# Input stage of a hybrid decoder layer: later scaling of constants, no GpSimd subtractions, casts on ScalarE, one product in fp32, a new order

## The chip, the cores and the metric

The kernel runs on one core of one Trainium2 chip. The metric is device time in microseconds; the time before is the median of three runs, 1275.76 us.

## The reference, cut to what matters

One layer of a decoder trunk with two token mixers side by side. The part that the change touches is the first: layer norm of the 16 meta tokens and 1024 tokens, and the first three of the products with `w_in`.

```python
D_MODEL, SEQ, N_META = 1024, 1024, 16                  # 1040 tokens in all
def reference(x, meta_tokens, in_ln_g, in_ln_b, ..., w_in, b_in, ...):
    h = jnp.concatenate([meta, x], axis=1)
    h = layer_norm(h, in_ln_g, in_ln_b)                # the input stage
    h = hybrid_layer(h, ...)
    return h[:, N_META:]

def hybrid_layer(h, ...):
    z = h @ w_in + b_in
    q, k, v, c_in, gates = jnp.split(z, ...)           # 512, 128, 128, 1024, 2048 columns
    a = swa_sink_attention(q, k, v, attn_sinks, rel_bias)
    y_attn = a @ w_attn_proj
    ...                                                # gated conv branch, merge, norm, conv FFN, norm
```

## The kernel before, in words

**Products in three parts.** Nearly every fp32 product is made of three TensorE products of rounded operands. An operand is split in a high part (a cast to the rounded type fp32r) and a low part (the operand minus the high part, again rounded); low x high, high x high and high x low are summed in PSUM. So each operand costs a cast and a subtraction before TensorE can use it. A product can also be made directly in fp32 from the raw operands, which takes no cast and no subtraction.

**The input stage.** Tokens come as nine tiles of up to 128 rows: the meta tokens (`xm`, tile -1) and eight tiles of x. `stat` takes the mean and variance of a tile on VectorE (L440, L441; `half_stat`, L452, does half a tile), `table` the reciprocal square root on ScalarE (L459), `newton` refines it in four small VectorE steps (L465 to L468), `norm` normalizes the tile on VectorE (L478) or ScalarE (L480). Statistics go in four sets: (-1), (0, 1), (2, 3, 4), (5, 6, 7). Three token groups of 272, 384 and 384 columns follow: (-1, 0, 1), (2, 3, 4), (5, 6, 7). For each group and each of eight channel chunks k, `turns` transposes on TensorE (L498, with the identity matrix, which comes in the tile `coll`), `scaled` applies gain and bias on ScalarE (L504, `FA` or `tm`, with columns of the tile `colr`), and `parts` makes the high part on VectorE (L514, into `RHO`) and the low part on VectorE (L519) or GpSimd (L517, into `RHC`).

**The first products.** `first` holds three weight tiles of 128 columns, in this order of indices: 0 the keys (column tile 4), 1 the values (column tile 5), 2 the first queries (column tile 0). `wsplit0(i)` splits one: a cast on ScalarE (L526), then a subtraction on GpSimd (L528; all three calls ask for it). `z_first(g, tiles, *ks)` makes the products of group g with the named tiles for chunks ks, three TensorE products for each k (L550), or one fp32 product where `raw` is set (L547: the keys of the first group). `evac` empties PSUM on ScalarE: keys (L379), values (L386), queries (L395 and L397, and a VectorE subtraction, L398); the stores of keys and of the queries' high part are issued from ScalarE's queue (L128).

**What sets the order.** Three lists, `dv`, `ac` and `pe`, pin the order of VectorE, ScalarE and TensorE in this stage to the order in which the program text issues the work; the sequence is written out by hand (L563 on). Evacuations are not pinned; they have a rank (`RK_EVAC`), and a scheduler places them. Loads are issued from SyncE (SP) in an order set by ranks; raw weights have two buffers (`wr`), and the fourth fill waits until one of the first is done with. The pools that matter: four PSUM buffers for transposes, four for normalized tiles, five for `tm`.

**Behind the stage.** The next weight tile (`wt_c1`, column tile 11) is split by ScalarE (L304) and VectorE (L307) into the buffer that the key weights leave, and the long run of products in `z_group` starts (L342, L345, L346). Beside it VectorE works off the residual rows (`residual`, L293 and L294), and later the convolution.

**The constants.** Three small VectorE steps scale constants in `colr` (L247, L249, L252). They are unpinned, and stand in the program text ahead of the stage.

Of the kernel before, what the change touches and what calls it, by code (L numbers as in the profile page):

```python
# [26 lines left out]
OP = mybir.AluOpType  # L27
# [10 lines left out]
HD = 64  # L38
# [74 lines left out]
def tile_hybrid_layer(  # L113
# [3 lines left out]
    nc = tc.nc  # L117
# [12 lines left out]
    def f32(ap):  # L130
        return ap.bitcast(F)
# [115 lines left out]
    nc.vector.tensor_scalar(qb, colA[:, 0:4], HD ** -0.5, None, OP.mult)  # L247

    nc.vector.tensor_scalar(colA[:, 10:30], colA[:, 10:30], 0.5, None, OP.mult)  # L249
    half_ = constr.tile([P, 1], F, name="half")  # L250
    nc.vector.memset(half_, 0.5)
    nc.vector.tensor_scalar(nsink, sink, -1.0, None, OP.mult)  # L252
# [28 lines left out]
    def h0(k, hl, a, b):  # L281
        return (RHO, RHC)[hl][:, k * T + a:k * T + b]
# [159 lines left out]

    half_st = {}
# [26 lines left out]
    def norm(t, j, on_dve):  # L470
        x_, n = src_of(j)
        i = tokens[t].index(j)
        mv, t_, r_, m_ = norms[t]
        xns[j] = sp.tile([P, D], F, name="xn", tag="xn", bufs=4) if j >= 0 else xm
        to = xns[j] if j >= 0 else xm[96:]
        for a in range(0, D, 512):
            if on_dve:
                dv(V.tensor_scalar(to[:, a:a + 512], x_[:, a:a + 512], r_[:n, i:i + 1], m_[:n, i:i + 1], OP.mult, OP.add))  # L478
            else:
                ac(nc.scalar.activation(to[:, a:a + 512], x_[:, a:a + 512], AF.Identity, bias=m_[:n, i:i + 1],  # L480
                                        scale=r_[:n, i:i + 1]))
        later.append((x_, mv[:n, i, 0:1], r_[:n, i:i + 1], n, j))
# [24 lines left out]
    def parts(g, *ks, hi_act=(), on_pool=()):  # L507
        a, b = HG[g]
        for k in ks:
            tm = tms[g, k]  # L510
            if k in hi_act:
                ac(nc.scalar.copy(h0(k, 0, a, b), tm))
            else:
                dv(V.tensor_copy(h0(k, 0, a, b), tm))  # L514
            x_ = (h0(k, 1, a, b), tm, f32(h0(k, 0, a, b)), OP.subtract)
            if k in on_pool:
                nc.gpsimd.tensor_tensor(*x_)  # L517
            else:
                dv(V.tensor_tensor(*x_))  # L519
# [4 lines left out]
    def wsplit0(i, on_pool=False):  # L524
        hi, lo, raw = first[i]
        ac(nc.scalar.copy(hi, raw))  # L526
        x_ = (lo, raw, f32(hi), OP.subtract)
        last_split.append(nc.gpsimd.tensor_tensor(*x_) if on_pool else dv(V.tensor_tensor(*x_)))  # L528
# [46 lines left out]
    norm(1, 1, False)  # L575
    turns(0, 0, 1, 2, 3)
    wsplit0(1, True)
    stat(2, 2, 3)
# [6 lines left out]
    parts(0, 0, 1)  # L585
    stat(2, 4)
    scaled(0, 5)
    wsplit0(2, True)
    scaled(0, 6, 7)
    z_first(0, (0,), 5, 6, 7, raw=True)  # L590
    table(2)
    parts(0, 2, 3, 4)
    newton(2)
    norm(2, 2, True)
    norm(2, 3, False)
    norm(2, 4, True)
    evac(0, 0)
    parts(0, 5, 6, 7)
    z_first(0, (1,), 0, 1)
    for k in range(2, 6):  # L600
        z_first(0, (1,), k)
        z_first(0, (2,), k - 2)
    turns(1, 0, 1, 2, 3)
    scaled(1, 0, 1, 2, 3)
    wsplit0(0, True)
    z_first(0, (1,), 6)
    z_first(0, (2,), 4)
    z_first(0, (1,), 7)
# [12 lines left out]
    parts(1, 4)  # L621
    half_stat(3, 6, 1)
    parts(1, 5)
    half_stat(3, 7, 0)
    parts(1, 6)
    half_stat(3, 7, 1)
    table(3)
    parts(1, 7)
# [1180 lines left out]
```

## Time and profile before

| | |
|---|---|
| median of 3 runs | 1275.76 us (1275.7 to 1277.3) |
| the profiled execution: its own time | 1277.78 us |
| its span, first to last instruction | 1276.0 us |
| mean granted TensorE clock | 0.994 |
| TensorE busy | 1255.9 us, 98% |
| VectorE busy | 1078.4 us, 85% |
| ScalarE busy | 587.0 us, 46% |
| GpSimd busy | 19.5 us, 2% |

Times are microseconds from the start of the span. PE is TensorE, PEld its weight loads, DVE VectorE, ACT ScalarE, POOL GpSimd, SP SyncE; a q behind the name is the engine's queue. A row of the timeline gives the start, the duration, the engine, the line, the operation, output and inputs, shapes and a count; what stands in brackets is the idle time before it and what ended that. A fp32 matmul shows as two records. TensorE's ends are modelled, so its durations overlap, and the pace is read from start to start.

### The profile page before, as it was taken

The numbers are of one execution on the slowest core, as the hardware profiler recorded it, in microseconds if no ns is written. First come the engines' busy times: TensorE is split into PE (matmuls) and PEld (weight loads), VectorE is DVE, ScalarE is ACT, GpSimd is POOL, SyncE is SP. The second block draws the span as 40 slices with busy tenths as digits, with TensorE's granted clock in tenths as the row PEclk, the third lists the DMA queues.
The fourth block names the chain that finished last, engine by engine and source line by source line (L and its number), as shares of the span: only waits on it lengthen the run. The fifth ranks groups of instructions, "written<-read, shape, count | busy, mean of one in ns | idle before, by whom it ended". The sixth has DMA issues, their size and how long they took to land.

```text
span 1276.0 us, 23038 instructions
## 1 busy us (share of the span) xinstructions
PE 1255.9 (98%) x9194; PEld 1185.9 (93%) x9194; DVE 1078.4 (85%) x1862; ACT 587.0 (46%) x1080; POOL 19.5 (2%) x16
## 2 busy tenths in 40 slices
PE   7999999999999999999999999999999999999997
PEld 6899999999999999788899999999999998788886
DVE  6889999999988476538899999999889886887697
ACT  4523344555564232345555454555455543536330
POOL 2200000001000000000000000000000000000000
PEclk8999999999999999999999999999999999999999
DMA  6275643423256465222145555553454566989712
GB/s 248 76 245 148 174 129 90 126 72 95 74 136 177 145 174 132 77 83 99 67 133 182 190 207 184 180 203 129 166 192 180 190 210 245 394 299 383 261 71 83
DMA packets 98701, 212.19 MB, mean 166 GB/s; under 512 B 11411, under 2 KB 38611, under 8 KB 98338
## 3 DMA queue, kind: packets, MB, share of 16 engines
q1 hardware_dynamic: 84474, 199.64, 46.9%
q10 hardware_dynamic: 14120, 11.08, 2.7%
q8 instruction: 72, 1.18, 0.4%
q14 instruction: 35, 0.29, 0.1%
HBM read 150.29 MB, written 62.70 MB: 167 GB/s over the span
## 4 chain that ended last, share of the span: by engine, by line
PE 88%; DVE 6%; DMA 2%; ACT 1%; issue 1%; SPq 1%; POOL 0%; DVEq 0%; ACTq 0%
PE px L1526 14%; PE py L1526 9%; PE ps_x L1655 9%; PE ps_z L342 8%; PE ps_z L346 7%; PE ps_z L345 7%; PE ps_z L1655 5%; PE pw L1526 5%; PE pz L1526 4%; PE ps_p L346 2%; PE ps_p L342 2%; PE ps_p L345 2%; PE ps_w L346 2%; PE ps_w L342 2%; PE ps_w L345 2%; PE ps_t L911 1%
## 5 line engine op out<-in xcount | busy, mean ns | idle before, releaser
L346 PE MATMUL ps_z<-RHC,w 128*128 128x256 f32 (+2 forms) x864 | 244.7, 283 | 0.0
L342 PE MATMUL ps_z<-RHO,w 128*128 128x256 f32 (+2 forms) x864 | 244.5, 283 | 0.1
L345 PE MATMUL ps_z<-RHO,w 128*128 128x256 f32 (+2 forms) x864 | 244.1, 282 | 0.0
L342 PEld LDWEIGHTS ps_z<-RHO,w 128*128 128x128 f32 x864 | 162.6, 188 | 1.7 <-ACT FA L697 0.7
L346 PEld LDWEIGHTS ps_z<-RHC,w 128*128 128x128 f32 x864 | 162.8, 188 | 0.6
L345 PEld LDWEIGHTS ps_z<-RHO,w 128*128 128x128 f32 x864 | 162.8, 188 | 0.6
L717 DVE SCALAR_TENSOR_TENSOR FA<-cin,cdw,FA 128x1026 f32<-128x1026 f32 x120 | 154.8, 1296 | 0.7
L1348 DVE TENSOR_TENSOR RHO<-wr,RHO 128x512 fp32r<-128x512 f32 x94 | 64.2, 691 | 6.8 <-ACT RHO L1347 6.6
L304 ACT CAST w<-wr 128x1024 fp32r<-128x1024 f32 x37 | 38.8, 1048 | 66.9 <-PE ps_z L346 47.9
L1347 ACT CAST RHO<-wr 128x512 fp32r<-128x512 f32 x94 | 56.7, 619 | 26.2 <-DVE wr L1365 12.2
L307 DVE TENSOR_TENSOR w<-wr,w 128x1024 fp32r<-128x1024 f32 x37 | 45.1, 1218 | 19.9 <-ACT w L304 19.8
L1365 DVE TENSOR_TENSOR wr<-wr 128x512 f32<-128x512 f32 x88 | 60.9, 692 | 0.1
L726 ACT ACTIVATE FA<-ps_z,colr 128x258 f32<-128x258 f32 (+1 forms) x64 | 30.2, 473 | 63.4 <-PE ps_z L346 49.8
L1348 DVE TENSOR_TENSOR w<-wr,w 128x512 fp32r<-128x512 f32 x60 | 40.9, 690 | 5.5 <-ACT w L1347 5.3
L1538 ACT COPY FA<-px 128x514 f32<-128x514 f32 (+2 forms) x23 | 13.1, 570 | 70.3 <-PE px L1526 70.3
L1347 ACT CAST w<-wr 128x512 fp32r<-128x512 f32 x60 | 36.3, 618 | 17.8 <-DMA wr<-in_w_up_dram 10.3
L1526 PE MATMUL px<-OA,RHO 128*128 128x258 f32 x324 | 43.2, 283 | 0.0
L1453 ACT ACTIVATE FA<-OB,coll 128x512 f32<-128x512 f32 x44 | 35.9, 815 | 15.1 <-DVE OB L1534 15.1
L1526 PE MATMUL px<-OC,RHO 128*128 128x256 f32 x324 | 41.5, 278 | 0.0
L1526 PE MATMUL px<-RHC,RHO 128*128 128x258 f32 (+1 forms) x312 | 41.1, 281 | 0.4 <-ACT OB L1538 0.4
L1538 ACT COPY OB<-px 128x514 f32<-128x514 f32 (+2 forms) x46 | 26.1, 566 | 31.8 <-PE px L1526 31.6
L1526 PEld LDWEIGHTS px<-OA,RHO 128*128 128x128 f32 x324 | 40.5, 189 | 0.2 <-ACT OB L1538 0.2
(441 smaller groups left out, 3317.0 us busy)
## 6 DMA issues: line engine op xcount, KB each, us to landing
wr<-in_w_up_dram SPq DMA_DIRECT2D x44, 512.0 KB, 3.6
wr<-in_w_z_dram SPq DMA_DIRECT2D x29, 512.0 KB, 4.3
fd<-FA SPq DMA_DIRECT2D x44, 256.0 KB, 2.1
OB<-in_w_down_dram SPq DMA_DIRECT2D x21, 512.0 KB, 4.9
FA<-sd SPq DMA_DIRECT2D x15, 512.0 KB, 8.8
qt<-qd SPq DMA_DIRECT2D x28, 256.0 KB, 4.9
sgd<-FA ACTq DMA_DIRECT2D x48, 128.0 KB, 2.7
td<-OB SPq DMA_DIRECT2D x12, 512.0 KB, 2.7
```

The source lines that it names most:

```text
L304: ins = nc.scalar.copy(hi, raw)
L307: return nc.vector.tensor_tensor(lo, raw, f32(hi), OP.subtract)
L342: ins = nc.tensor.matmul(ps, al, bh, start=i == 0, stop=False)
L345: nc.tensor.matmul(ps, ah, bh, start=False, stop=False)
L346: last = nc.tensor.matmul(ps, ah, bl, start=False, stop=i == n - 1)
L717: nc.vector.scalar_tensor_tensor(acc[c], cin[:, j:j + U], wc, acc[c], OP.mult, OP.add)
L1347: nc.scalar.copy(hi, src)
L1348: ins = nc.vector.tensor_tensor(lo, src, f32(hi), OP.subtract)
L1365: ins = nc.vector.tensor_tensor(*x)
L1526: ins = nc.tensor.matmul(o, x[:, ks], bmat(sub, q, hl, k), start=first and k + j == 0, stop=k == 3 and j == 2, skip_group_check=not first)
L1538: copied.append(nc.scalar.copy(*x))
L1655: nc.tensor.matmul(banks[i], l[:, ts], r[:, ws], start=first and a and x + k == 0, stop=z and x == len(ops) - 1 and k == 2, skip_group_che ...
```

## The change

The three scalings of constants become pinned steps (`scales`), behind the normalization of the first x tiles. `parts` is taken apart into `high` (on ScalarE, or on VectorE where asked) and `low` (on VectorE); `wsplit0` is taken apart into `whigh` (ScalarE) and `wlow` (VectorE). Nothing of the stage is left on GpSimd. The values' product of the first group is made in fp32 from the raw weights. The high parts of the first group (but for chunk 0) and of the second are cast by ScalarE; those of the third stay on VectorE. The order by hand is new: the splits of the weights come later (query weights, then value weights, then key weights, the last behind the second group's low parts), the second set's statistics are spread differently, and the queries' product of the first group comes behind four of the second group's transposes.

```diff
-    nc.vector.tensor_scalar(qb, colA[:, 0:4], HD ** -0.5, None, OP.mult)
-    nc.vector.tensor_scalar(colA[:, 10:30], colA[:, 10:30], 0.5, None, OP.mult)
...
-    nc.vector.tensor_scalar(nsink, sink, -1.0, None, OP.mult)
...
+    def scales():
+        dv(V.tensor_scalar(qb, colA[:, 0:4], HD ** -0.5, None, OP.mult))
+        dv(V.tensor_scalar(colA[:, 10:30], colA[:, 10:30], 0.5, None, OP.mult))
+        dv(V.tensor_scalar(nsink, sink, -1.0, None, OP.mult))
...
-    def parts(g, *ks, hi_act=(), on_pool=()):
+    def high(g, *ks, on_dve=False):
         a, b = HG[g]
         for k in ks:
-            ...
+            if on_dve:
+                dv(V.tensor_copy(h0(k, 0, a, b), tms[g, k]))
             else:
-                dv(V.tensor_copy(h0(k, 0, a, b), tm))
-            x_ = (h0(k, 1, a, b), tm, f32(h0(k, 0, a, b)), OP.subtract)
-            if k in on_pool:
-                nc.gpsimd.tensor_tensor(*x_)
-            else:
-                dv(V.tensor_tensor(*x_))
+                ac(nc.scalar.copy(h0(k, 0, a, b), tms[g, k]))
+
+    def low(g, *ks):
+        a, b = HG[g]
+        for k in ks:
+            dv(V.tensor_tensor(h0(k, 1, a, b), tms[g, k], f32(h0(k, 0, a, b)), OP.subtract))
+
+    def parts(g, *ks):
+        for k in ks:
+            high(g, k, on_dve=True)
+            low(g, k)
...
-    def wsplit0(i, on_pool=False):
+    def whigh(i):
+        ac(nc.scalar.copy(first[i][0], first[i][2]))
+
+    def wlow(i):
         hi, lo, raw = first[i]
-        ac(nc.scalar.copy(hi, raw))
-        x_ = (lo, raw, f32(hi), OP.subtract)
-        last_split.append(nc.gpsimd.tensor_tensor(*x_) if on_pool else dv(V.tensor_tensor(*x_)))
+        last_split.append(dv(V.tensor_tensor(lo, raw, f32(hi), OP.subtract)))
...
     norm(1, 1, False)
+    scales()
     turns(0, 0, 1, 2, 3)
-    wsplit0(1, True)
-    stat(2, 2, 3)
+    stat(2, 2)
     scaled(0, 0)
     z_first(0, (0,), 0, raw=True)
     for k in range(4):
         scaled(0, k + 1)
         turns(0, k + 4)
         z_first(0, (0,), k + 1, raw=True)
-    parts(0, 0, 1)
+    parts(0, 0)
+    scaled(0, 5, 6, 7)
+    z_first(0, (0,), 5, 6, 7, raw=True)
+    evac(0, 0)
+    stat(2, 3)
     stat(2, 4)
-    scaled(0, 5)
-    wsplit0(2, True)
-    scaled(0, 6, 7)
-    z_first(0, (0,), 5, 6, 7, raw=True)
+    whigh(1)
     table(2)
-    parts(0, 2, 3, 4)
+    z_first(0, (1,), *range(8), raw=True)
+    evac(0, 1)
     newton(2)
     norm(2, 2, True)
+    norm(2, 4, True)
+    whigh(2)
     norm(2, 3, False)
-    norm(2, 4, True)
-    evac(0, 0)
-    parts(0, 5, 6, 7)
-    z_first(0, (1,), 0, 1)
-    for k in range(2, 6):
-        z_first(0, (1,), k)
-        z_first(0, (2,), k - 2)
+    wlow(2)
+    high(0, *range(1, 8))
+    low(0, *range(1, 8))
     turns(1, 0, 1, 2, 3)
     scaled(1, 0, 1, 2, 3)
-    wsplit0(0, True)
-    z_first(0, (1,), 6)
-    z_first(0, (2,), 4)
-    z_first(0, (1,), 7)
-    evac(0, 1)
-    z_first(0, (2,), 5)
+    z_first(0, (2,), *range(8))
+    evac(0, 2)
+    wlow(1)
     turns(1, 4, 5, 6, 7)
-    z_first(0, (2,), 6, 7)
-    evac(0, 2)
-    parts(1, 0, 1)
-    scaled(1, 4, 5, 6, 7)
-    half_stat(3, 5, 0)
-    parts(1, 2)
-    half_stat(3, 5, 1)
-    parts(1, 3)
+    stat(3, 5)
+    high(1, 0, 1, 2, 3)
+    low(1, 0, 1)
+    scaled(1, 4)
     half_stat(3, 6, 0)
-    parts(1, 4)
+    low(1, 2)
+    scaled(1, 5)
+    high(1, 4)
     half_stat(3, 6, 1)
...
+    high(1, 6, 7)
     half_stat(3, 7, 1)
+    low(1, 5)
     table(3)
-    parts(1, 7)
+    low(1, 6, 7)
+    whigh(0)
+    wlow(0)
     newton(3)
     norm(3, 5, True)
     norm(3, 6, False)
     norm(3, 7, True)
     for k in range(8):
         z_first(1, (1, 2), k)
     evac(1, 1, 2)
-    z_first(1, (0,), 0, 1)
+    z_first(1, (0,), 0, 1, 2)
     turns(2, 0, 1, 2, 3)
     scaled(2, 0, 1, 2, 3)
-    parts(2, 0, 1, 2, 3, on_pool=(1, 3))
-    z_first(1, (0,), 2, 3, 4, 5)
+    parts(2, 0, 1, 2, 3)
+    z_first(1, (0,), 3, 4, 5)
     turns(2, 4, 5, 6, 7)
     scaled(2, 4, 5, 6, 7)
-    parts(2, 4, 5, 6, 7, on_pool=(5, 7))
+    parts(2, 4, 5, 6, 7)
     z_first(1, (0,), 6, 7)
     evac(1, 0)
     for i in range(3):
         z_first(2, (i,), *range(8))
         evac(2, i)
```

More of the change, by code (lines that the diff above doesn't have):

```diff
@@ L584, in tile_hybrid_layer @@
         z_first(0, (0,), k + 1, raw=True)
-    parts(0, 0, 1)
+    parts(0, 0)
[3 more added lines that the diff above has]
+    stat(2, 3)
     stat(2, 4)
-    scaled(0, 5)
-    wsplit0(2, True)
-    scaled(0, 6, 7)
-    z_first(0, (0,), 5, 6, 7, raw=True)
+    whigh(1)
     table(2)
-    parts(0, 2, 3, 4)
+    z_first(0, (1,), *range(8), raw=True)
+    evac(0, 1)
     newton(2)
     norm(2, 2, True)
+    norm(2, 4, True)
+    whigh(2)
     norm(2, 3, False)
-    norm(2, 4, True)
-    evac(0, 0)
-    parts(0, 5, 6, 7)
-    z_first(0, (1,), 0, 1)
-    for k in range(2, 6):
-        z_first(0, (1,), k)
-        z_first(0, (2,), k - 2)
+    wlow(2)
+    high(0, *range(1, 8))
+    low(0, *range(1, 8))
     turns(1, 0, 1, 2, 3)
     scaled(1, 0, 1, 2, 3)
-    wsplit0(0, True)
-    z_first(0, (1,), 6)
-    z_first(0, (2,), 4)
-    z_first(0, (1,), 7)
-    evac(0, 1)
-    z_first(0, (2,), 5)
-    turns(1, 4, 5, 6, 7)
-    z_first(0, (2,), 6, 7)
-    evac(0, 2)
-    parts(1, 0, 1)
-    scaled(1, 4, 5, 6, 7)
-    half_stat(3, 5, 0)
-    parts(1, 2)
-    half_stat(3, 5, 1)
-    parts(1, 3)
+    z_first(0, (2,), *range(8))
+    evac(0, 2)
+    wlow(1)
+    turns(1, 4, 5, 6, 7)
+    stat(3, 5)
+    high(1, 0, 1, 2, 3)
+    low(1, 0, 1)
+    scaled(1, 4)
     half_stat(3, 6, 0)
-    parts(1, 4)
+    low(1, 2)
+    scaled(1, 5)
+    high(1, 4)
     half_stat(3, 6, 1)
-    parts(1, 5)
+    low(1, 3)
+    scaled(1, 6)
+    high(1, 5)
     half_stat(3, 7, 0)
-    parts(1, 6)
+    low(1, 4)
+    scaled(1, 7)
+    high(1, 6, 7)
     half_stat(3, 7, 1)
+    low(1, 5)
     table(3)
-    parts(1, 7)
+    low(1, 6, 7)
+    whigh(0)
+    wlow(0)
     newton(3)
```

3 lines of the change are left out of this document (removed).

## The prediction

> **What bounds the kernel now.** The page comes first, for the span, then the busy time by stretches, for the place.
>
> ```profile
> span 1276.0 us, 23038 instructions
> ...
> core 0: us, PE busy (x) PEld busy (x) DVE busy (x) ACT busy (x) POOL busy (x), PEclk, DMA share, GB/s
> 20.00:30.00 10.00, 7.97 (x51) 7.28 (x50) 8.63 (x21) 3.42 (x7) 2.61 (x1) 0.92 0.30 116
> 30.00:40.00 10.00, 9.81 (x61) 9.27 (x60) 8.97 (x16) 6.81 (x12) 2.40 (x1) 0.90 0.22 66
> 40.00:50.00 10.00, 9.79 (x54) 7.98 (x54) 8.46 (x24) 5.19 (x10) 0.00 (x0) 1.00 0.09 26
> ...
> 60.00:70.00 10.00, 10.00 (x71) 10.00 (x70) 9.96 (x9) 3.91 (x5) 0.00 (x0) 1.00 0.68 181
> ...
> 25.08:28.49 3.41, 1.38 (x10) 1.14 (x10) 3.34 (x9) 1.43 (x2) 0.00 (x0) 1.00 0.00 0
> 28.49:31.90 3.41, 3.41 (x19) 3.41 (x17) 1.46 (x5) 1.75 (x4) 0.00 (x0) 0.50 0.00 0
> 10.00:60.00 50.00, 44.68 (x250) 39.79 (x251) 41.55 (x91) 27.88 (x48) 11.55 (x7) 0.90 0.37 137
> ```
>
> From 60 us on TensorE (PE) has no gap: 10.00 of 10. The change touches only what lies ahead of that, and there PE is either idle (7.97 of 10 in 20 to 30), or busy by count but not by pace: 54 records in 40 to 50 against 61 and 71 in its neighbours. So the question is when the long run of products (L342) begins. In the timeline of PE:
>
> ```profile
> 10.62 0.30 PE L498 MATMUL ps_h<-coll,xm 128*128 128x128 f32 x1 [3.15 <-ACT xm L480]
> 12.96 0.48 PE L498 MATMUL ps_h<-coll,xn 128*128 128x128 f32 x1 [2.04 <-DVE xn L478]
> ...
> 20.14 2.00 PE L547 MATMUL ps_z<-FA,wr 128*128 128x272 f32 x8
> ...
> 27.17 0.52 PE L550 MATMUL ps_z<-RHO,w 128*128 128x272 f32 x2 [2.03 <-DVE RHO L514]
> ...
> 34.67 0.52 PE L550 MATMUL ps_z<-RHO,w 128*128 128x384 f32 x2
> ...
> 35.20 0.51 PE L550 MATMUL ps_z<-RHO,w 128*128 128x384 f32 x2
> ...
> 46.38 1.47 PE L498 MATMUL ps_h<-coll,xn 128*128 128x128 f32 x12
> 47.61 0.59 PE L550 MATMUL ps_z<-RHO,w 128*128 128x384 f32 x2
> ...
> 65.32 0.29 PE L342 MATMUL ps_z<-RHO,w 128*128 128x272 f32 x1
> ```
>
> The keys' product of the first group ends at 22.1. At 27.17 PE had waited 2.03 us for a high part from VectorE. The second group begins at 34.67. Three products of 384 columns pace at 0.53 us (34.67 to 35.20), twelve transposes at 1.23 (46.38 to 47.61). From 34.67 on there are 48 such threes, 25.4 us, and two lots of transposes, 2.5: 27.9 in all. The stretch to 65.32 is 30.65 long, so 2.75 us in it are stalls. Both stalls come from VectorE (DVE):
>
> ```profile
> 9.31 0.17 DVE L247 TENSOR_SCALAR qb<-colr 128x4 f32<-128x4 f32 x1 [2.12 <-DMA colr<-in_cols_dram]
> ...
> 12.36 1.00 DVE L478 TENSOR_SCALAR xn<-x,r,m 128x512 f32<-128x512 f32 x2
> ...
> 15.70 1.29 DVE L440 BATCH_NORM_STATS2 st<-x 128x6 f32<-128x512 f32 x2 [0.89 <-DMA x<-in_x_dram]
> ...
> 20.63 2.49 DVE L514 CAST RHO<-FA 128x272 fp32r<-128x272 f32 x1
> ...
> 24.21 0.16 DVE L465 SCALAR_TENSOR_TENSOR t<-mv,r 128x3 f32<-128x3 f32 x1
> ...
> 33.57 2.78 DVE L519 TENSOR_TENSOR RHC<-tm,RHO 128x384 fp32r<-128x384 f32 x1
> ...
> 44.38 0.15 DVE L465 SCALAR_TENSOR_TENSOR t<-mv,r 128x3 f32<-128x3 f32 x1
> ...
> 20.36 2.61 POOL L528 TENSOR_TENSOR w<-OB,w 128x1024 fp32r<-128x1024 f32 x1 [3.05 <-ACT w L526]
> 33.53 2.40 POOL L528 TENSOR_TENSOR w<-wr,w 128x1024 fp32r<-128x1024 f32 x1 [10.56 <-ACT w L526]
> ```
>
> The cast at 20.63 took 2.49 us where its kind takes 0.29, and the subtraction at 33.57 took 2.78; each began inside a GpSimd subtraction (20.36 to 22.97, 33.53 to 35.93) and ended with it. So DVE loses some 2.2 us to each. It also waits 2.12 us at 9.31 for `colr`, for a scaling that nobody needs yet.
>
> **The change part by part.** The prices, one row for each kind:
>
> ```profile
> L514 DVE CAST RHO<-tm 128x384 fp32r<-128x384 f32 x16 | 5.2, 342 | 3.0 <-ACT tm L504 3.0
> ...
> L519 DVE TENSOR_TENSOR RHC<-FA,RHO 128x272 fp32r<-128x272 f32 x8 | 3.5, 443 | 0.3
> ...
> L452 DVE BATCH_NORM_STATS2 st<-x 128x6 f32<-128x512 f32 x6 | 4.1, 684 | 0.0
> ...
> L478 DVE TENSOR_SCALAR xn<-x,r,m 128x512 f32<-128x512 f32 x10 | 4.8, 544 | 0.2
> ...
> L307 DVE TENSOR_TENSOR w<-wr,w 128x1024 fp32r<-128x1024 f32 x1 | 1.2, 1226 | 2.7 <-ACT w L304 2.7
> ...
> L526 ACT CAST w<-wr 128x1024 fp32r<-128x1024 f32 x2 | 2.1, 1046 | 0.0
> ...
> L397 ACT CAST qsh<-FA 128x384 fp32r<-128x384 f32 x1 | 0.5, 503 | 0.0
> ...
> L397 ACT CAST qsh<-FA 128x258 fp32r<-128x258 f32 x1 | 0.4, 400 | 0.0
> ...
> L504 ACT ACTIVATE tm<-ps_h,colr 128x384 f32<-128x384 f32 x16 | 9.7, 670 | 4.9 <-PE ps_h L498 4.3 <-DVE RHC L519 0.5
> ...
> 30.15 2.36 ACT L504 ACTIVATE tm<-ps_h,colr 128x384 f32<-128x384 f32 x4 [3.64 <-PE ps_h L498]
> ...
> 37.44 0.81 ACTq L128 DMA_DIRECT2D qd<-qsh  x2
> ...
> 6.72 0.33 SPq L124 DMA_DIRECT2D x<-in_x_dram  x1
> ...
> SPq L124 <- DMA x<-in_x_dram: 0.7, 1, 0.7
> ```
>
> *Scalings put off.* Without the wait, DVE's next work (the statistics of the second x tile) can start at 7.2 instead of 9.3 us, if that tile has landed. SyncE's queue was held for an x tile until its issue at 6.72, and the tile in question is by its place in the order the second, so I take it as landed; if not, the gain shrinks at most to nothing. The identity, for the transposes, is there by 10.62, where the meta tile is transposed with it. So the normalization at 12.36 comes at 10.2, the transposes at 12.96 come at 10.8, and the keys' product ends at 20.0 instead of 22.1. The three scalings themselves then stand behind that normalization, where DVE soon waits for x again (0.89 us at 15.70): free, and their first reader is the queries' evacuation, past 26.
>
> *Values in fp32.* Four fp32 products of 272 columns took 2.00 us (20.14), so eight take at most 4.0, against 8 x 0.53 x 272/384 = 3.0 in three parts. It costs 1.0 us of PE and takes away every wait for split value weights and for low parts. PE is through at 24.0.
>
> *Statistics and norms of the second set.* The fourth x tile still lands at 15.70; two tiles' statistics (1.29 for the two halves and some 0.2 for the merge) end at 18.7, if the fifth (issued behind the second, 6.72) has landed by 17.2; a later landing is covered by the 1.5 us that PE comes after ACT below. Before, four pairs of parts (4 x 0.73 = 2.9) and the GpSimd stall (2.2) stood between that work and the Newton steps at 24.21: 24.2 - 5.1 = 19.1. With 0.8 for Newton and four halves at 0.54 the DVE tiles are ready at 22. ScalarE (ACT) has to fit two weight casts (2 x 1.05) around its own tile and is done by 22.5. PE arrives at 24.0, so this is off the path, and its transposes end at 25.2. The queries' product of the first group (3.0 us) follows and fills PE to about 28.
>
> *Casts on ScalarE.* This now sets the start of the second group. ACT from 22.5: a values' evacuation (0.5), seven casts of 272 columns (0.40 alone; ACT instructions in a row overlap by 0.08, since four scalings of 0.67 took 2.36 at 30.15; so 0.33), 25.3; four scalings, 2.4, 27.7; the queries' evacuation, about 0.9 (an activation and a cast of 258 columns), with two store issues, 0.8 (37.44), 29.4; the first cast of 384 columns, 0.50, 29.9. DVE's subtraction takes 0.443 at 272 columns, so about 0.6 at 384: the second group starts at 30.5 instead of 34.67.
> The evacuation is not pinned; if it lands elsewhere the start is 28.8, if its issues are held, later. A wide cast costs 0.50 on ACT against 0.34 on DVE, so the eight of the second group cost 8 x 0.16 = 1.3 us more in all. I don't book these 1.3, since the engine that PE waited for is DVE, and the casts now run beside its subtractions; they count in the bounds.
> The Trainium skill speaks against such a move (ScalarE: Activation LUTs, section "Rules for kernel authors": plain elementwise arithmetic belongs on VectorE, which is faster per element). By that rule alone the 1.3 would be booked, and the forecast would be 1271.5; on the order of the two prices the trace agrees.
>
> *Second and third group.* PE needs 1.06 us for a chunk of values and queries. ACT needs 0.59 + 0.42 for a chunk's scaling and cast, DVE 0.6 + 0.68 with half a tile's statistics in four chunks: 4 x 0.22 = 0.9 us of stall is left of the 2.75. The key weights' split comes last: ACT's last cast is through at 29.9 + 7 x 0.42 + 4 x 0.59 = 35.2, then a root (0.3), the cast (1.05), the subtraction (1.23): 37.8. PE gets there at 30.5 + 8.5 + 0.9 = 39.9, so 2.1 us of cover; were it gone, each us counts in full. Newton and the first norm of the third set then end at 39.7, ahead of the transposes at 41.5. The third group's parts cost DVE 0.34 + 0.6 a chunk; eight from 43.5 on end at 51.0, while PE wants the last at 50.4: 0.4 with the rounding. Without the GpSimd subtractions, nothing holds DVE there.
> The raw buffers come free later (value weights with the subtraction at about 27, key weights at 37.8). SyncE's queue, with the next weights and the queries' low stores behind it, waits that long; the first of these weights is wanted 8 us before L342, so past 50: hidden.
>
> *The sum.* 30.5 + 27.9 + 0.9 + 0.4 = 59.7 for the first L342, against 65.3: 5.6 us earlier. Behind it PE has no gap to give the gain to, and DVE comes to its residual rows as much earlier. The profiled execution took 1277.78 us, 2.0 above the median of the runs and 1.8 above its own span; it would take 1272.2, and the median becomes 1275.76 - 5.6 = 1270.2. Ends of the unknown costs: evacuation elsewhere and no stall, 3.0 better; a later landing of the second x tile, nothing (the wait at 15.70 hides it); all fifteen casts without the overlap of 0.08 (1.2) and the 1.3 not booked, 2.5 worse.
>
> **The rivals.** *The clock drops.* In 25.08 to 28.49 PE was busy 1.38 of 3.41 us, and in the next 3.41 us the granted clock was 0.50. After the change PE has a hole of 2.5 us around 28 to 30.5. If it is read the same way, the second group runs 3.4 us at half speed and loses 1.7: 5.6 - 1.7 = 3.9, so 1271.9. For: the same share of idleness. Against: PE is busy up to 28, and the hole may be cut by a boundary.
> The Trainium skill has this as a rule (TensorE: Matmul & The Clock Gate, part 1: a free-running window of about 3.4 us of idleness halves the clock); the two rows agree.
>
> *ScalarE in series, slower than before.* ACT is busy 27.88 of 50 us in 10 to 60, and the change adds 7 x 0.40 + 8 x 0.50 = 6.8. If the casts don't run beside DVE's work but in a ring (transposes wait for PSUM that the scalings free, these stand behind casts, and those behind evacuations), then 6.8, the key weights' split (2.3), 1.0 of fp32 and 1.7 of clock, 11.8 in all, stand against 2.1 + 2.0 + 2.75 = 6.9 of stalls: 4.9 slower, 1280.7. The point from which it decides: Newton of the third set later than today's 44.38, that is the last low part of the second group later than 42; my sum has it at about 36. Against: two fifths of ACT's time there is idle.
>
> *Given back.* The products behind 60 us wait for something that doesn't move, a load or the residual rows: 1275.8. For: DVE is busy 9.96 of 10 in 60 to 70. Against: PE shows 10.00 there, and DVE starts as much earlier.
>
> **How the numbers follow.** Forecast (1266.8 to 1271) 0.46, clock 0.22, other smaller gains (to 1274: a held store, a longer ring) 0.12, given back 0.08, slower 0.10, better than 1266.8 0.02. The range 1266.8 to 1274.0 holds the first three, 0.80. About 0.2%, 2.6 us, is what a measurement can tell here; it cuts the third case at 1273.2. Faster 0.80, same 0.10, slower 0.10.
>
> **What would show it.** The first L342 near 59.7; no DVE cast or subtraction over 1 us in 15 to 55; first x transposes at 10.8; second group from 30.5, its stretch to L342 some 29 us; a granted clock of 1.00 from 28 on, or else 0.5 for 3.4 us. Wrong: ACT idle near nothing in 25 to 40, L342 later than 63, or L342 early and an end that isn't.

## The result and the profile after

| | before | after |
|---|---|---|
| median, runs of one chip | 1276.96 us (1275.7 to 1279.47) | 1271.08 us (1269.82 to 1271.92) |
| span of the profiled execution | 1276.0 us | 1269.3 us |
| mean granted TensorE clock in it | 0.994 | 0.995 |

After to before is 0.9951, with a 95% interval of 0.9937 to 0.9966: the medians are 5.9 us apart, where 5.6 were forecast. A second series gave 1270.38 against 1277.15, 0.9948 (0.9934 to 0.9962).

Busy time by stretches of the input stage, kernel after (columns: stretch, length, busy time and instructions of PE, PEld, DVE, ACT, POOL, granted clock, DMA share, GB/s):

```profile
20.00:30.00 10.00, 10.00 (x71) 9.33 (x70) 9.93 (x21) 10.00 (x24) 0.00 (x0) 1.00 0.36 128
30.00:40.00 10.00, 10.00 (x63) 9.85 (x62) 8.96 (x22) 7.28 (x16) 0.00 (x0) 1.00 0.28 80
...
10.00:60.00 50.00, 48.73 (x296) 46.11 (x297) 43.17 (x89) 35.51 (x65) 0.00 (x0) 0.97 0.52 174
```

Where PE had 7.97 of 10 in 20 to 30, it now has 10.00, with 71 records for 51. The clock is full there. The engines that feed PE are full instead: DVE 9.93 and ACT 10.00 in 20 to 30. The timeline of PE, kernel after:

```profile
11.12 0.43 PE L499 MATMUL ps_h<-coll,xn 128*128 128x128 f32 x1 [2.05 <-DVE xn L479]
...
17.40 5.67 PE L553 MATMUL ps_z<-FA,wr 128*128 128x272 f32 x24
22.91 1.47 PE L499 MATMUL ps_h<-coll,xn 128*128 128x128 f32 x12
...
27.08 1.47 PE L499 MATMUL ps_h<-coll,xn 128*128 128x128 f32 x12
28.30 0.60 PE L556 MATMUL ps_z<-RHO,w 128*128 128x384 f32 x2
...
56.84 0.29 PE L338 MATMUL ps_z<-RHO,w 128*128 128x272 f32 x1
```

Line numbers have moved: L547 is now L553, L550 is L556, L342 is L338. No row behind 11.12 has a bracket, so PE waits for nothing from there to the long run of products. That run begins at 56.84 instead of 65.32, 8.5 us earlier, and the span is only 6.7 shorter. The rest was given back far behind the stage, in the down projection. There, a stretch of five us in the kernel before (columns as above):

```profile
1084.00:1089.00 5.00, 3.49 (x15) 2.27 (x14) 2.67 (x3) 2.09 (x2) 0.00 (x0) 1.00 1.04 406
```

The waits of PE in the first 42 us of the down projection, kernel before (who waits for whom: us in total, times, longest):

```profile
PE ps_x L1655 <- ACT RHO L1617: 1.0, 1, 1.0
PE ps_x L1655 <- DVE RHO L1618: 0.5, 1, 0.5
```

The stretches of the kernel after at that place, and then its waits:

```profile
1075.00:1080.00 5.00, 2.85 (x13) 2.08 (x12) 1.54 (x2) 2.09 (x2) 0.00 (x0) 0.96 1.03 403
1080.00:1085.00 5.00, 4.97 (x16) 3.47 (x15) 2.87 (x4) 2.10 (x2) 0.00 (x0) 0.70 1.05 387
```

```profile
PE ps_x L1663 <- ACT RHO L1625: 2.1, 1, 2.1
```

Before, PE waits 1.5 us there at full clock. After, it waits 2.1, and the clock then drops: 0.70 in the mean of the next five. The first part of the down projection, up to a marked product some 37 us in, takes 39.6 us for 37.5. Of the other stretches none differs by more than 0.8 us: from the first long product to the attention 93.1 and 93.2, from there to the means 201.5 and 202.3, to the last of the `w_in` products 67.4 and 66.7, to the up projection 191.8 and 191.7, the up projection itself 437.1 and 436.8, the rest of the down projection 173.9 in both, and 8.4 to the end in both.

### The profile page after: what moved, and what is told of

The parts are those of the page before. It is cut to its first block, busy times and chain, and to the rows that moved or that the text cites. A ratio compares the mean times of both kernels' runs of the same rounds, so it can differ in the third digit from the quotient of the medians.

```text
span 1269.3 us, 23031 instructions
## 1 busy us (share of the span) xinstructions
PE 1252.8 (99%) x9186; PEld 1184.5 (93%) x9186; DVE 1073.1 (85%) x1854; ACT 591.6 (47%) x1095; POOL 8.1 (1%) x9
## 4 chain that ended last, share of the span: by engine, by line
PE 93%; DVE 2%; DMA 2%; ACT 2%; issue 1%; SPq 0%; DVEq 0%; ACTq 0%
PE px L1534 14%; PE py L1534 10%; PE ps_x L1663 9%; PE ps_z L338 8%; PE ps_z L342 8%; PE ps_z L341 8%; PE pw L1534 5%; PE pz L1534 5%; PE ps_z L1663 5%; PE ps_p L342 2%; PE ps_p L338 2%; PE ps_p L341 2%; PE ps_w L342 2%; PE ps_w L338 2%; PE ps_w L341 2%; PE ps_z L556 2%
## 5 line engine op out<-in xcount | busy, mean ns | idle before, releaser
L342 PE MATMUL ps_z<-RHC,w 128*128 128x256 f32 (+2 forms) x864 | 244.6, 283 | 0.0
L338 PE MATMUL ps_z<-RHO,w 128*128 128x256 f32 (+2 forms) x864 | 244.4, 283 | 0.2 <-ACT FA L734 0.2
L338 PEld LDWEIGHTS ps_z<-RHO,w 128*128 128x128 f32 x864 | 162.6, 188 | 2.0 <-ACT FA L705 0.7
L342 PEld LDWEIGHTS ps_z<-RHC,w 128*128 128x128 f32 x864 | 162.7, 188 | 0.4
L1534 PE MATMUL px<-OC,RHO 128*128 128x256 f32 x324 | 41.5, 277 | 0.0
```

The source lines that it names most:

```text
L338: ins = nc.tensor.matmul(ps, al, bh, start=i == 0, stop=False)
L342: last = nc.tensor.matmul(ps, ah, bl, start=False, stop=i == n - 1)
L1534: ins = nc.tensor.matmul(o, x[:, ks], bmat(sub, q, hl, k), start=first and k + j == 0, stop=k == 3 and j == 2, skip_group_check=not first)
```

## The experiments

"Long run" is the start of the first long product, "down" the length of the first part of the down projection, "half clock" the time at a granted clock of 0.5 from 7 to 40 us and in that part of the down projection: these three from the profiled execution. Each ratio is to runs of the kernel before in the same series; differences between two kernels, below, are given as a range over after's two series.

| kernel | median us | to before (95%) | long run | down | half clock |
|---|---|---|---|---|---|
| before | 1276.96 | | 65.3 | 37.5 | 10.2 + 0 |
| before, second trace | 1276.75 | 1.0002 (0.9991 to 1.0012) | 63.7 | 38.1 | 6.8 + 0 |
| b_scales | 1277.79 | 1.0004 (0.9995 to 1.0013) | 63.8 | 39.3 | 6.8 + 3.4 |
| b_no_pool | 1279.68 | 1.0023 (1.0014 to 1.0032) | 64.4 | 40.2 | 3.4 + 3.4 |
| after | 1271.08 | 0.9951 (0.9937 to 0.9966) | 56.8 | 39.6 | 3.4 + 3.4 |
| after, second trace | 1270.38 | 0.9948 (0.9934 to 0.9962) | 55.3 | 38.4 | 0 + 0 |
| a_scales_first | 1273.5 | 0.9967 (0.9954 to 0.9979) | 59.4 | 40.3 | 6.8 + 3.4 |
| a_pool_weights | 1273.63 | 0.9974 (0.9964 to 0.9984) | 59.6 | 39.6 | 3.4 + 3.4 |
| a_casts_dve | 1274.74 | 0.9977 (0.9968 to 0.9986) | 59.0 | 41.3 | 3.4 + 6.8 |
| a_values_split | 1273.62 | 0.9969 (0.9958 to 0.9981) | 58.2 | 41.5 | 3.4 + 6.8 |
| a_warm36 | 1270.81 | 0.9947 (0.9935 to 0.996) | 56.0 | 40.8 | 0 + 3.4 |
| a_gains_late | 1270.86 | 0.9945 (0.9929 to 0.9961) | 56.5 | 39.6 | 3.4 + 3.4 |
| a_sums_late | 1266.69 | 0.9917 (0.9904 to 0.9931) | 56.4 | 36.2 | 3.4 + 0 |
| a_both_late | 1267.01 | 0.9919 (0.9905 to 0.9933) | 56.9 | 36.1 | 3.4 + 0 |

Except in the last three kernels, the code of the down projection is the same in all, and its first part still takes from 37.5 to 41.5 us: 37.5 to 38.4 without a window at half clock, 39.3 to 40.8 with one, 41.3 and 41.5 with two. So a difference between two times isn't made in the input stage alone; the column "long run" gives the stage's part of it, in one execution of each.

### One part of the change alone, in the kernel before

**b_scales**: only the three scalings put off.

```diff
-    nc.vector.tensor_scalar(qb, colA[:, 0:4], HD ** -0.5, None, OP.mult)
-    nc.vector.tensor_scalar(colA[:, 10:30], colA[:, 10:30], 0.5, None, OP.mult)
-    nc.vector.tensor_scalar(nsink, sink, -1.0, None, OP.mult)
...
     norm(1, 1, False)
+    scales()
```

> The kernel before, with the three scalings of constants put off and nothing else. Theory 1 (the second token group's start is set by VectorE, which waits for the fourth x tile at 15.7 and then has its parts and the GpSimd stalls before it): first x transposes 2 us earlier, keys' product ends 2 us earlier, but L342 starts within 0.5 us of 65.3 and the time is that of before. Theory 2 (the early wait is itself a good part of the gain): L342 at about 63.2, 2 us faster.

No gain: 1.0004. The transposes come at 10.79 instead of 12.96, and the long run begins at 63.8 instead of 65.3, with one half-clock window less. But the second trace of before, with the scalings still in front, has nearly the same. Its timeline of VectorE, and then of PE:

```profile
7.48 0.17 DVE L247 TENSOR_SCALAR qb<-colr 128x4 f32<-128x4 f32 x1 [0.29 <-DMA colr<-in_cols_dram]
```

```profile
11.14 0.43 PE L498 MATMUL ps_h<-coll,xn 128*128 128x128 f32 x1 [2.04 <-DVE xn L478]
```

There VectorE waited 0.29 us for `colr`, not 2.12, the transposes came at 11.14 and the long run began at 63.7. So how long the scalings hold VectorE differs between executions of the same kernel, and from this pair of traces b_scales gains 0.35 us at the transposes and nothing at the long run: PE still waits 2.0 us for a high part from VectorE behind the first group, and 1.0 more for ScalarE's first scaled chunk. Whether a full 2 us would be lost again in the old order isn't shown; between the two traces of before, a start 1.8 us earlier went with a long run 1.6 us earlier.

**b_no_pool**: the seven GpSimd subtractions of the stage moved to VectorE, in the same order.

```diff
-    wsplit0(1, True)
+    wsplit0(1)
...
-    parts(2, 0, 1, 2, 3, on_pool=(1, 3))
+    parts(2, 0, 1, 2, 3)
```

> The kernel before, with the seven subtractions of GpSimd done by VectorE in the same order, and nothing else. Theory 1: VectorE takes on 3 x 1.22 + 4 x 0.56 = 5.9 us and loses stalls of 2.2 + 2.2 + 3 x 0.7 = 6.5, so L342 comes 0 to 1.3 us earlier (64.0 to 65.3) and the gain is at most 1.3. Theory 2 (the stalls are the gain): L342 near 61, 4 us faster.

Slower, 1.0023, which neither theory had. Timeline of VectorE, this kernel, and then the waits of PE from 10 to 66:

```profile
31.46 1.23 DVE L528 TENSOR_TENSOR w<-wr,w 128x1024 fp32r<-128x1024 f32 x1 [3.78 <-ACT w L526]
32.60 0.35 DVE L514 CAST RHO<-tm 128x384 fp32r<-128x384 f32 x1
```

```profile
PE ps_z L550 <- DVE RHO L514: 3.9, 3, 2.0
```

The operations stretched to 2.5 us are gone, but the key weights' subtraction now stands in VectorE's own line. There it waits 3.78 us for ScalarE's cast, with the second group's parts behind it. PE's waits for high parts go from 2.0 us to 3.9. In the trace the long run still begins at 64.4, between the two traces of before, with less time at half clock than either; the rest of the loss lies in the down projection, 40.2 us with one half-clock window. So the new waits eat up what the stage gained, and the stage is not faster without GpSimd in this order; how the 2.9 us between its median and that of before in the same series (1276.8) divide isn't settled.

### One part undone, in the kernel after

**a_scales_first**: the scalings back in their old place.

```diff
+    nc.vector.tensor_scalar(qb, colA[:, 0:4], HD ** -0.5, None, OP.mult)
...
     norm(1, 1, False)
-    scales()
```

> The changed kernel, with the three scalings back at the front. Theory 1 (after the change TensorE runs without a gap from 11.1 us to the first long product, so a later start counts in full): x transposes at 13, L342 at 58.8 to 59.5 instead of 56.8, some 2 us slower than the changed kernel, 3.5 to 4 us faster than before. Theory 2 (as the prediction had it, the wait for x hides the start): L342 at 56.8, no difference.

1273.5: 2.4 us slower than after's first series, 3.1 than its second. Timeline of VectorE, this kernel:

```profile
8.82 0.17 DVE L247 TENSOR_SCALAR qb<-colr 128x4 f32<-128x4 f32 x1 [1.66 <-DMA colr<-in_cols_dram]
...
15.80 1.28 DVE L440 BATCH_NORM_STATS2 st<-x 128x6 f32<-128x512 f32 x2
```

Its timeline of PE:

```profile
12.48 0.48 PE L498 MATMUL ps_h<-coll,xn 128*128 128x128 f32 x1 [2.05 <-DVE xn L478]
```

And the timeline of VectorE, kernel after:

```profile
14.99 1.29 DVE L436 BATCH_NORM_STATS2 st<-x 128x6 f32<-128x512 f32 x2 [0.39 <-DMA x<-in_x_dram]
```

The wait for `colr` is back (1.66) and the transposes are 1.4 later than the 11.12 of after. Nothing absorbs it: in after VectorE waited only 0.39 us for the fourth x tile, and here not at all. PE then runs without a wait to the long run, at 59.4. The profiled execution had a second half-clock window as well; how the 2.4 to 3.1 divide between the later start and the clock isn't settled. Nor is it known how often the wait for `colr` comes: it was 2.12 and 0.29 us in the two traces of before, and one of the five executions here took 1270.39, as long as after.

**a_pool_weights**: the three weight subtractions back on GpSimd.

```diff
-        last_split.append(dv(V.tensor_tensor(lo, raw, f32(hi), OP.subtract)))
+        last_split.append(nc.gpsimd.tensor_tensor(lo, raw, f32(hi), OP.subtract))
```

> The changed kernel, with the three weights' subtractions back on GpSimd (2.4 us each instead of 1.22 on VectorE). Theory 1: VectorE's subtractions beside them are held until each ends, by up to 2.2 us; the queries' product of the first group waits about 1 us, the key weights come 1.2 us later; L342 at 57.8 to 60, 1 to 3 us slower than the changed kernel. Theory 2 (GpSimd is off the path here): within 0.5 us of the changed kernel.

2.6 to 3.3 us slower than after. Timeline of GpSimd, this kernel, then that of VectorE, then the waits of PE from 10 to 60:

```profile
17.51 2.36 POOL L534 TENSOR_TENSOR w<-wr,w 128x1024 fp32r<-128x1024 f32 x1 [14.20 <-ACT w L530]
19.84 2.34 POOL L534 TENSOR_TENSOR w<-OB,w 128x1024 fp32r<-128x1024 f32 x1
```

```profile
17.60 2.29 DVE L466 SCALAR_TENSOR_TENSOR t<-mv,r 128x3 f32<-128x3 f32 x1 [0.47 <-ACT r L460]
19.93 2.27 DVE L467 SCALAR_TENSOR_TENSOR t<-t,r 128x3 f32<-128x3 f32 x1
```

```profile
PE ps_h L499 <- DVE xn L479: 3.8, 2, 2.0
```

Two Newton steps on three columns, 0.16 us each, take 2.29 and 2.27: each begins inside a GpSimd subtraction and ends with it. Newton is thereby 4.2 us longer, and PE waits twice for a norm, 3.8 us in all, where after has only the one at 11.12. The long run begins at 59.6 for after's 56.8, and the down projection takes 39.6 as there: the loss is made in the stage. GpSimd's price is what it holds on VectorE, not its own time. The Trainium skill (SBUF — State Buffer, section "SBUF: two separate sides") has it as an exclusive lock on a port that GpSimd shares with VectorE steps of two inputs; these rows agree.

**a_casts_dve**: the fifteen casts back on VectorE, in the new order.

```diff
-    high(0, *range(1, 8))
+    high(0, *range(1, 8), on_dve=True)
...
-    high(1, 0, 1, 2, 3)
+    high(1, 0, 1, 2, 3, on_dve=True)
```

> The changed kernel, with the fifteen casts of the first two groups back on VectorE. Theory 1 (VectorE is the full engine between 20 and 30 us, 9.93 of 10 busy): 7 x 0.30 + 8 x 0.35 = 4.9 us more on it, L342 at 59.5 to 62 instead of 56.8, 3 to 5 us slower than the changed kernel. Theory 2 (by the rule of the Trainium skill, ScalarE: Activation LUTs, rules for kernel authors: VectorE is the better place): no slower, or up to 1.3 us faster.

3.7 to 4.4 us slower than after. Busy time from 20 to 30, this kernel, and then the waits of PE from 10 to 60:

```profile
20.00:30.00 10.00, 7.99 (x58) 6.98 (x57) 10.00 (x28) 4.96 (x10) 0.00 (x0) 1.00 0.38 130
```

```profile
PE ps_z L556 <- DVE RHO L512: 1.3, 1, 1.3
PE ps_z L556 <- DVE RHC L519: 0.7, 1, 0.7
```

DVE is full, 10.00 of 10, ACT half empty, 4.96, and PE is back at 7.99. A cast costs half as much again on ACT (in a row 0.33 and 0.44 us in after, against 0.22 and 0.28 on DVE in this kernel) and is worth moving all the same, since the engine that PE waits for is DVE. The time is theory 1's; the long run, at 59.0, is 0.5 earlier than it said. Of the loss, 2.1 us (3.7 against after's second trace) are made in the stage, the rest in the down projection, which had two half-clock windows here. So the rule of the Trainium skill that plain arithmetic belongs on VectorE (ScalarE: Activation LUTs, "Rules for kernel authors") gives the right order of the prices and the wrong time here.

**a_values_split**: the values' product in three parts again.

```diff
-    z_first(0, (1,), *range(8), raw=True)
-    evac(0, 1)
...
-    z_first(0, (2,), *range(8))
-    evac(0, 2)
+    z_first(0, (1, 2), *range(8))
+    evac(0, 1, 2)
```

> The changed kernel, with the values' product of the first group in three parts again, beside the queries' product, and the value weights' subtraction ahead of it. Theory 1 (the fp32 product costs 8 x (0.46 - 0.38) = 0.65 us but keeps TensorE busy while the low parts are made): TensorE has a hole of some 3 us around 20, L342 2 to 4 us later than 56.8, and so much slower than the changed kernel. Theory 2 (it only costs): 0.65 us faster.

The value weights' subtraction also moves ahead of that of the query weights. 2.5 to 3.2 us slower, as theory 1 has it. Without the fp32 product PE has nothing to do while the second set is normalized. Its timeline, this kernel, and then two stretches:

```profile
19.67 0.32 PE L499 MATMUL ps_h<-coll,xn 128*128 128x128 f32 x1 [1.98 <-DVE xn L479]
```

```profile
16.41:19.82 3.41, 1.43 (x7) 0.87 (x5) 2.87 (x10) 2.95 (x6) 0.00 (x0) 1.00 1.05 398
19.82:23.22 3.40, 3.15 (x15) 2.98 (x15) 3.40 (x6) 3.40 (x10) 0.00 (x0) 0.50 0.55 207
```

The fp32 product takes more of PE's time than the three parts, but it needs no operand from VectorE, and it stood where PE had to wait. The hole is 1.98 us, not 3, and it also cost a window at half clock. The long run comes at 58.2: 1.4 us behind after's first trace and 2.9 behind its second, where 2 to 4 were expected; the two half-clock windows of the down projection are the rest.

**a_warm36**: 36 products on constants ahead of the stage instead of 20, to keep PE busy before the first transposes.

```diff
-    for i in range(20):
+    for i in range(36):
```

> The changed kernel with 36 instead of 20 warming products on TensorE, to about 9.8 us. Theory 1 (the clock of 0.5 from 11.4 to 14.8 comes of the idle stretch from 7.5 on, and TensorE bounds the stage): granted clock near 1.00 from 11.4 on, keys' product 1 to 1.5 us earlier, L342 0.5 to 1.5 us earlier, as much faster. Theory 2 (the stretch up to 23 us is covered by the wait for x tiles, the statistics and the norms of the second set): clock back, L342 unchanged within 0.3.

All five executions had a mean clock of 0.997 or more, the traced one has no half-clock window at the start, and the time is after's, as theory 2 has it: 1270.81. The transposes come at 11.56, 0.4 to 0.7 later than in after, and the long run at 56.0, between after's 56.8 and 55.3. Why the full clock brings nothing in the time isn't settled: the start is later, and the first part of the down projection took 40.8 us in this trace.

### Where 2.1 us were given back

**after_again**: the kernel after, unchanged, in a second series.

> The changed kernel once more, on the chip of these runs, for its trace. Theory 1 (what is given back behind L342 comes of a wait for loads in the down projection, after which the granted clock halves for one window in some executions): L342 at 56.8 again; if the granted clock dips in the down projection the span is near 1269.3, if not, near 1268. Theory 2 (the loss is a fixed one): the same 2.1 us lost between 1070 and 1087 without a dip.

1270.38, 0.9948: the same gain. The trace has no window at half clock. The span is then 1266.9, 1.1 less than theory 1 has without a dip, since the long run begins at 55.3 and not at 56.8 again. A fixed loss, theory 2, it is not: the first part of the down projection takes 38.4 us, not 39.6.

**before_again**: the kernel before, unchanged, traced a second time.

> The kernel before, unchanged: a second trace of it, to part what the change did from what the clock happened to do in the first trace. Theory 1 (the first trace of before lost time at the start to three windows at half clock and had none in the down projection, both by chance of where the windows fall): the first long product comes between 62.6 and 64.6 and not at 65.32, and from there to the end it is 1211.5 to 1213.5 us and not 1210.7; the mean granted clock stays at 0.994 to 0.996. Theory 2 (the kernel before is like that whatever the windows): first long product 65.3 within 0.3, and 1210.7 within 0.3 behind it.

The long run begins at 63.73, as theory 1 has it, and the rest takes 1211.1 us, between the theories' figures: 0.4 more than in the first trace. The windows at half clock differ from execution to execution of one kernel, so the size of the gain in one pair of traces is partly theirs. But both pairs give the same at the start, 65.3 to 56.8 and 63.7 to 55.3, and 6.7 and 7.9 us in the spans. In both, after has 6.8 us less at half clock at the start, two windows: one follows PE's wait of 2.0 us for a high part, which the change takes away, the other lies ahead of 18.3. Half of 6.8, so 3.4 us at most (an estimate, for a PE that is busy throughout), is what the clock gives of the stage's 8.5. Three stretches of after:

```profile
11.22:14.63 3.41, 3.38 (x13) 2.79 (x14) 2.63 (x9) 2.36 (x6) 0.00 (x0) 0.50 1.02 414
...
1076.17:1079.58 3.41, 1.39 (x7) 0.81 (x5) 1.18 (x1) 2.02 (x2) 0.00 (x0) 1.00 1.03 402
1079.58:1083.00 3.42, 3.26 (x7) 2.15 (x8) 1.97 (x3) 0.48 (x2) 0.00 (x0) 0.50 1.05 386
```

Two stretches of its second trace, and then the longer wait of PE in the first 42 us of the down projection there:

```profile
1074.49:1077.91 3.42, 1.80 (x8) 1.14 (x7) 0.97 (x1) 1.81 (x2) 0.00 (x0) 1.00 1.04 410
1077.91:1081.32 3.41, 2.55 (x10) 1.81 (x11) 2.17 (x3) 0.47 (x2) 0.00 (x0) 1.00 1.04 387
```

```profile
PE ps_x L1663 <- ACT RHO L1625: 2.0, 1, 2.0
```

The second trace has the same wait (and 0.5 us more for VectorE) and, from 1065 to 1110, no drop. In the first, 1079.58 less 11.22 is 313.0 times 3.413 us: the clock changes on a grid that goes on by itself. In the second trace the granted clock rises at 6.12 and falls at 1262.22, behind the last product, and does not change in between; those two are 368.0 cells of the grid apart, so its cells can be laid as well, and the two stretches shown are cells. The wait is cut there by the boundary at 1077.91, and PE is busy 1.80 and 2.55 us in the two. All fourteen traces, up to the end of the products, say the same: of 25 cells at full clock in which PE was busy 1.72 us or less, 24 are followed by one at half clock (the other, of 1.64, is the first cell in a_pool_weights), and of those with 1.75 or more none is. So what decides is how much of a wait falls into one cell. The Trainium skill (TensorE: Matmul & The Clock Gate, part 1) calls this a free-running window of 3413 ns; these rows agree on its length, and a window need not be idle throughout to halve the clock.

**a_gains_late**: the loads of two gain rows, 1 MB, moved from the second step of the down projection to the fourth.

```diff
-    steps([(sums_load, FC - 2)], [(gain_rows, 0)], [(sums_last, FC - 2), (row, 4, 0)], ...
+    steps([(sums_load, FC - 2)], [], [(sums_last, FC - 2)], [(gain_rows, 0)], [(row, 4, 0), (row, 5, 0)], ...
```

> The kernel after, with the load of the first two gain rows (two broadcast loads of 512 KB) moved from the second to the fourth step of the down projection, and the residual rows 4 to 7 behind it. After lost 2.1 us against before in the first 37 us of that stage, where TensorE waited 2.1 us for a cast on ScalarE whose load came late and the clock then fell to 0.5 for 3.4 us. Theory 1 (these loads stand in the queue ahead of the operands' loads and make them late): the wait goes below 0.7 us, the first 37 us of the stage go from 39.6 to 37.5 or less, no half clock behind it, and the kernel is 1 to 3 us faster than after: 1268 to 1270. Theory 2 (the DMA engines are full there whatever the order, share 1.05): the wait stays at 1.5 to 3 us or moves to the place of the loads, and the time stays at 1270.4 to 1271.2.

Theory 2's outcome: 1270.86, the wait 2.1 as before. The trace of after says why. Its timeline of SyncE's queue (start and duration of the issue), and then of ACT, with the cast that PE waits for:

```profile
1067.88 0.85 SPq L124 DMA_DIRECT2D w<-fd  x2
1068.78 0.43 SPq L124 DMA_DIRECT2D FA<-fd  x1
1069.31 0.82 SPq L124 DMA_DIRECT2D OB<-in_w_down_dram  x1
1070.23 2.55 SPq L124 DMA_DIRECT2D w<-in_ln_dram  x2
```

```profile
1078.61 1.04 ACT L1625 CAST RHO<-OB 128x1024 fp32r<-128x1024 f32 x1 [0.24 <-DMA OB<-in_w_down_dram]
```

The gain rows (`in_ln`) are issued behind the weights `OB` that PE waits for. What is issued ahead of them is `w<-fd`, the two blocks of the next sums, 1 MB too.

**a_sums_late** and **a_both_late**: these two blocks moved from the first step to the third, alone and with the gain rows.

```diff
-    steps([(sums_load, FC - 2)], [(gain_rows, 0)], [(sums_last, FC - 2), (row, 4, 0)], ...
+    steps([], [(gain_rows, 0)], [(sums_load, FC - 2), (row, 4, 0)], [(row, 5, 0)], [(sums_last, FC - 2), (row, 6, 0)], ...
```

> The kernel after, with the load of the next sums' two blocks (2 x 512 KB) moved from the first to the third step of the down projection, their sums from the third to the fifth. In the trace of after these loads are issued at 1067.88, ahead of the features' and weights' loads at 1068.78 and 1069.31 whose cast TensorE then waited 2.1 us for; DMA moved 327 to 403 GB/s there, so 1 MB is 2.6 to 3.2 us. Theory 1 (the loads are served in the order of their issue, and these two made the operand late; the gain rows, issued behind the operand, could not): the wait of TensorE goes below 0.6 us, the first 37 us of the stage from 39.6 to 36 to 37.6, no half clock in it, the kernel 1 to 3 us faster than after. Theory 2 (there is too much to load in these steps whatever the order): a wait of over 1 us comes at another operand, and the time stays within 0.7 us of after's 1270.4 to 1271.1.

> The kernel after, with both moved: the sums' two blocks to the third step, the gain rows to the fourth, the residual rows 4 to 7 to the fifth and sixth. Theory 1: as a_sums_late on the first operand, and more room at the second, so no wait over 0.3 us in the first 37 us, 36 to 37 us for them, 1267.5 to 1269.5 in all. Theory 2: the wait returns later, at the rows or where 3 MB meet in the fifth and sixth steps, and the time is that of after or up to 2 us more.

Theory 1 in both, with more than it said: 1266.69 and 1267.01, where at least 1267.4 and 1267.5 were expected. The same two timelines of a_sums_late, and then PE's waits:

```profile
1068.17 0.40 SPq L124 DMA_DIRECT2D OB<-in_w_down_dram  x1
1068.67 1.10 SPq L124 DMA_DIRECT2D w<-in_ln_dram  x2
```

```profile
1075.76 1.05 ACT L1625 CAST RHO<-OB 128x1024 fp32r<-128x1024 f32 x1 [0.18 <-DMA OB<-in_w_down_dram]
```

```profile
PE ps_x L1663 <- DVE RHO L1626: 0.5, 1, 0.5
```

The cast comes at 1075.76 instead of 1078.61, 2.9 us earlier (0.2 of it by an earlier start of the down projection), within the 2.6 to 3.2 worked out for 1 MB. The wait of 2.1 is gone, so is the half-clock window, and the first part of the down projection takes 36.2 us instead of 39.6. What is left, 0.5 and in a_both_late 0.4 us for VectorE, is a little over the 0.3 expected of the latter. Moving the gain rows as well adds nothing that can be told. This version beats both kernels: 10.7 us under before, 3.7 to 4.4 under after. The kernel before has a wait at the same place (1.5 us in its first trace, 2.1 in its second); that it would gain from the same edit wasn't tried.

## Why the prediction was right, and where its steps were not

**Right in the main.** The end of the stage sets the time, and the gain is made there: waits of PE for VectorE go, by taking casts and GpSimd's holds off VectorE. a_casts_dve and a_pool_weights show both parts. That 5.6 us were forecast and 5.9 measured is luck in part, since two errors offset each other: the stage gained 8.5 us in the traces and not 5.6, and part of that was given back behind it (1.8 us in the first pair of traces, 0.5 in the second; in the executions without a trace it isn't known). The 0.9 us between 1270.2 and the median are of another kind: the median of before went from 1275.76, of three runs, to 1276.96, of five. With 1271.08 the result stands at the upper edge of the band that the prediction gave its forecast (to 1271).

**Scalings.** Transposes were put at 10.8; they came at 11.12, and at 10.86 in the second trace. But the 2.1 us that the sum books for it are what one execution waited: the second trace of before has its transposes at 11.14 with the scalings in front, and its long run still begins 8.4 us behind that of after's second trace. Another step that failed is the bound beside it, that a later landing would cost nothing because the wait at 15.70 hides it. In after that wait is 0.39 us; no run has a later landing alone, but a_scales_first, with a later start, cost 2.4 to 3.1.

**Values in fp32.** 4.0 us were allowed; the run of 24 records, twelve products, from 17.40 to 22.91 paces at 0.46, so eight take 3.7. PE was through at 22.9, not 24.0. Besides, the second clock window of before (to 18.25) didn't come in after, so the keys were done nearly a microsecond ahead of the 20.0 of the sum.

**Casts on ScalarE.** Its prices held, and the order failed. Timeline of ACT, kernel after:

```profile
21.94 2.33 ACT L514 CAST RHO<-FA 128x272 fp32r<-128x272 f32 x7
24.17 0.49 ACT L382 ACTIVATE FA<-ps_z,colr 128x272 f32<-128x272 f32 x1
24.55 2.34 ACT L505 ACTIVATE tm<-ps_h,colr 128x384 f32<-128x384 f32 x4
26.77 1.76 ACT L514 CAST RHO<-tm 128x384 fp32r<-128x384 f32 x4
28.42 0.49 ACT L391 ACTIVATE FA<-ps_z,qb 128x258 f32<-128x258 f32 x1
```

Seven casts take 2.33 (2.3 were reckoned) and four scalings 2.34 (2.4). But the queries' evacuation, which the sum put ahead of the first wide cast with 1.7 us, comes behind four of them, at 28.42. The second group begins at 28.3, not 30.5. The prediction named 28.8 for this case and took the other. And it isn't ACT any more that sets this start: from 22.91 on PE has two lots of transposes and the queries' product, row after row without a wait, up to 28.30. The prediction had left the second lot, 1.2 us (27.08 to 28.30), out of PE's work: by its own figures PE was through at 29.4, not 28, the hole was 1.1 us and not 2.5, and no order of ACT could have brought the start to 28.8.

**Stalls of the second and third group.** 0.9 and 0.4 were booked; from 28.30 to 56.84 are 28.54 us for 27.9 of work, so 0.6 at most. A half tile's statistics between the low parts (0.68) fit in, since the first lows are ahead of PE. The key weights' split ended at 36.1 (37.8 reckoned), the third group's parts at 47.7 (51.0): timeline of VectorE, kernel after.

```profile
34.85 1.23 DVE L534 TENSOR_TENSOR w<-wr,w 128x1024 fp32r<-128x1024 f32 x1
35.99 0.15 DVE L466 SCALAR_TENSOR_TENSOR t<-mv,r 128x3 f32<-128x3 f32 x1
...
47.12 0.56 DVE L519 TENSOR_TENSOR RHC<-tm,RHO 128x384 fp32r<-128x384 f32 x1
```

So these two are 1.7 and 3.3 us ahead of the sum's figures, and PE waits for neither.

**The rivals.** The clock didn't drop at 28 to 30.5, since the hole never opened. In the first trace it dropped in the down projection, where the prediction had seen no wait: "behind it PE has no gap" was read from a stretch that ends at 70 us. So a part of the third rival came true, by another way than its two candidates: not a load that stays where it was, but the order of loads in a full DMA, and a clock window. ScalarE in series didn't come: ACT was busy 7.6 us more in 10 to 60 (6.8 reckoned), and Newton of the third set stood at 35.99, far from the deciding 44.38.

## What to carry to other kernels

Price a move between engines by who is waited for, not by which engine does the operation faster: casts dearer by half on ScalarE were worth about 4 us, because VectorE was full. The parts of such a change need each other: taking GpSimd out alone made the kernel slower, and undoing any one part in the new order cost 2.4 us or more. Take a second trace of the kernel before, too: a wait of 2.12 us, on which a part of the forecast was built, was 0.29 in it. And when less comes out than the stage gave, look for the stretch of the span that got longer: here one stretch led to one load, whose place in the queue is worth some 4 us.

## What was not expected of the hardware

A GpSimd subtraction stretched VectorE steps on three columns from 0.16 to 2.29 us; small steps are held as long as large ones. A wait of 2 us was enough to lose a window of 3.4 us at half clock (PE busy 1.39 and 1.43 of 3.41 in the cells before), and where it falls on the grid decides: cut by a boundary, the same wait left 1.80 and 2.55 us and the clock stayed. Of 73 executions of the kernel before, those with a mean clock of 0.994 took 1278.3 us on average (24), those with 0.995 and 0.996 1276.4 (45).
